# Fourteen small DMAs ahead of the direct copies of a sliding-window kernel

## The chip, the cores and the metric

The kernel runs on one core of one Trainium2 chip. The time is the device time of one execution in microseconds (us); a profiled execution also has a span, from its first to its last instruction. The core has 16 DMA engines. Two queues feed them here, one that SyncE (SP) issues to and one that ScalarE (ACT) issues to, and the profile lists them as q1 (SP) and q10 (ACT). No compute engine does any work on the data.

## The reference

The input is `x` of 32 batches, 4096 rows and 256 columns in float32. The result holds, for each batch, 127 windows of 64 rows that start every 32 rows:

```python
n_windows = (length - window_size) // stride + 1        # 127
for i in range(n_windows):
    start = i * stride
    result[:, i] = x[:, start:start + window_size].copy()
```

It is a pure copy. One block is 32 rows of 256 numbers, 32 KB, and it lies in one piece in memory. A window is two neighbouring blocks, 64 KB, also in one piece in `x` and in `out`. Neighbouring windows overlap by one block, so the result is twice as large as the input: 266.3 MB are written.

## The kernel before, in words

The 32 batches are divided between two paths, each with a queue of its own; the two share nothing but the 16 DMA engines and the memory.

**Direct** (class `Direct`, lines 36 to 57, on SP's queue) does the first 21 batches from memory to memory. `windows` (line 42) issues one DMA for `n` windows. Its outer dimension is the window, its inner one the 64 KB of a window, and `max_dma_last_dim` cuts the inner one into pieces: 16 KB where `size` is `DIRECT`, 32 KB where it is `2 * DIRECT`. `run` (line 52) does, for each batch, seven DMAs of 16 windows (112 windows, four pieces of 16 KB each) and then a remainder of 15 windows in two pieces of 32 KB each (line 57). That makes 147 DMAs of 16 windows and 21 remainders. No wait stands between them: SP issues as fast as its queue takes them.

**Staged** (class `Staged`, lines 60 to 107, on ACT's queue) does the last 11 batches over on-chip memory. A load (line 79) brings 16 blocks of 32 KB into one of 24 slots, one block in each of 16 partitions. A store (line 91) writes each slot twice, once as the first half of 16 windows and once as the second half of the windows before them. At the ends of a batch one of the two has only 15 blocks, which is 22 of the 176 stores. `run` (line 101) issues ten loads ahead (`LEAD`), then in turn one load and the two stores of an earlier slot. A load of a slot that is used again waits for both stores of it, and a store waits for its load.

Every DMA that nothing else waits for adds 16 to the semaphore `done` (`count`, line 31), and SP waits for the sum of these at the end (line 131).

The order of the work is the order of the program text on each queue; nothing plans it. Direct's first DMA is the one of windows 0 to 15 of batch 0, and batch 0's remainder is its eighth.

Of the kernel before, what the change touches and what calls it, by code (L numbers as in the profile page):

```python
# [1 line left out]

# [4 lines left out]


DIRECT, STAGE = 16384, 16384
N_STAGED = 11  # L10
N_TILES = 6
LEAD = 10


class Geometry:


    def __init__(self, tc, x, out, B, L, D, W, S, n_win):
        assert W == 2 * S and L % S == 0 and n_win == L // S - 1
        self.x, self.out = x, out  # L20
        self.blk, self.nb, self.nw = S * D, L // S, n_win
        self.done, self.total = tc.alloc_semaphore("done"), 0

    def xap(self, b, block, dims):
        return bass.AP(self.x.tensor, self.x.offset + (b * self.nb + block) * self.blk, dims)

    def oap(self, b, w, half, dims):
        at = ((b * self.nw + w) * 2 + half) * self.blk
        return bass.AP(self.out.tensor, self.out.offset + at, dims)

    def count(self, dma):
        dma.then_inc(self.done, 16)
        self.total += 16


class Direct:


    def __init__(self, g, batches):
        self.g, self.batches = g, batches  # L40

    def windows(self, q, b, w0, n, size):
        g = self.g
        g.count(
            q.dma_start(
                out=g.oap(b, w0, 0, [[2 * g.blk, n], [1, 2 * g.blk]]),
                in_=g.xap(b, w0, [[g.blk, n], [1, 2 * g.blk]]),
                max_dma_last_dim=size,
            )
        )  # L50

    def run(self, q):
        full = self.g.nw // 16 * 16
        for b in self.batches:
            for w0 in range(0, full, 16):
                self.windows(q, b, w0, 16, DIRECT)
            self.windows(q, b, full, self.g.nw - full, 2 * DIRECT)


class Staged:  # L60

    def __init__(self, g, tc, pool, dtype, batches, n_tiles):
        self.g = g
        tiles = [pool.tile([128, g.blk], dtype, name=f"xb{i}") for i in range(n_tiles)]
        self.slots = [t[32 + c : 96 : 4, :] for t in tiles for c in range(4)]
        self.loaded = [tc.alloc_semaphore(f"loaded{i}") for i in range(len(self.slots))]  # L70
        self.stored = [tc.alloc_semaphore(f"stored{i}") for i in range(len(self.slots))]
        self.groups = [(b, j) for b in batches for j in range(0, g.nb, 16)]

    def load(self, q, r):
        g, (b, j) = self.g, self.groups[r]
        n, i = divmod(r, len(self.slots))
        if n:
            q.wait_ge(self.stored[i], 32 * n)
        q.dma_start(
            out=self.slots[i], in_=g.xap(b, j, [[g.blk, 16], [1, g.blk]]),  # L80
            max_dma_last_dim=STAGE,
        ).then_inc(self.loaded[i], 16)

    def store(self, q, r):
        g, (b, j) = self.g, self.groups[r]
        n, i = divmod(r, len(self.slots))
        q.wait_ge(self.loaded[i], 16 * (n + 1))
        for half in (0, 1):
            lo = 1 if half and j == 0 else 0
            hi = 15 if not half and j + 16 == g.nb else 16  # L90
            dma = q.dma_start(
                out=g.oap(b, j + lo - half, half, [[2 * g.blk, hi - lo], [1, g.blk]]),
                in_=self.slots[i][lo:hi, :],
                max_dma_last_dim=STAGE,
            )
            if r + len(self.slots) < len(self.groups):
                dma.then_inc(self.stored[i], 16)
            else:
                g.count(dma)

    def run(self, q, lead):
        for r in range(lead):
            self.load(q, r)
        for r in range(len(self.groups)):
            if r + lead < len(self.groups):
                self.load(q, r + lead)
            self.store(q, r)


@with_exitstack  # L110
def kernel(
    ctx: ExitStack,
    tc: tile.TileContext,
    x: bass.AP,
    window_size: bass.AP,
    stride: bass.AP,
    out: bass.AP,
):
    nc = tc.nc
    W, S = int(window_size), int(stride)  # L120
    B, L, D = x.shape
    n_win = (L - W) // S + 1
    assert out.shape == (B, n_win, W, D)
    g = Geometry(tc, x, out, B, L, D, W, S, n_win)
    pool = ctx.enter_context(tc.tile_pool(name="xb", bufs=1))
    staged = Staged(g, tc, pool, x.dtype, range(B - N_STAGED, B), N_TILES)
    direct = Direct(g, range(B - N_STAGED))
    with tc.tile_critical():
        staged.run(nc.scalar, LEAD)
        direct.run(nc.sync)  # L130
        nc.sync.wait_ge(g.done, g.total)


# [1 line left out]
_INS = ['x', 'window_size', 'stride']  # L135
_OUTS = [((32, 127, 64, 256), 'float32')]

_NUMBERS = {'window_size': 64, 'stride': 32}


# [26 lines left out]
```

## Time and profile before

| What | Value |
|---|---|
| Time, median of 4 runs | 763.61 us (763.14 to 764.68) |
| The profiled execution's own time | 764.08 us |
| Its span | 762.3 us |
| Bytes moved by the DMA engines | 312.53 MB, mean 410 GB/s |
| Read from and written to the chip's memory | 220.92 MB and 266.34 MB, 639 GB/s over the span |
| Direct, SP's queue (q1) | 12705 packets, 174.80 MB |
| Staged, ACT's queue (q10) | 12606 packets, 137.71 MB |
| DMAs issued: direct of 16 windows, direct remainders | 147, 21 |
| DMAs issued: loads, stores of 16 blocks, stores of 15 blocks | 88, 154, 22 |
| Busy compute engines | POOL 0.2 us, four constants at the start |

A packet is one contiguous piece that one DMA engine moves, or the four bytes with which an engine adds to a semaphore after its part of a DMA. The DMA line of the profile cuts the span into 40 slices and gives the mean busy share of the 16 engines, in tenths. In a table of stretches of time the share is given in hundredths: 0.94 is what 15 busy engines of 16 make, 0.06 is one of 16. A share slightly over 1 is possible because the records of one packet and the next on an engine overlap by a few ns.

### The profile page before, as it was taken

Reading aid. Unit: us, or ns where it says so; the run is one execution under the profiler, and the core shown is the slowest. Engines: PE = TensorE matmul, PEld = TensorE weight load, DVE = VectorE, ACT = ScalarE, POOL = GpSimd, SP = SyncE. Lnnn points to the kernel's source line nnn. Section 1 sums busy time; section 2 is a strip of 40 time slices with the busy share of each in tenths; the row PEclk is TensorE's granted clock in tenths of the full one; section 3 lists DMA queues with packets and bytes.
Section 4 is the critical chain, followed back from the end, with each engine's and each line's share of the span. In section 5 each row is a group of like instructions: output and inputs, shape, how many; then the busy total and the mean of one; then the engine's idle time right before and its main releaser. Section 6 shows DMA issues by size and latency. Waiting matters only on the chain. (4 is left out here: it accounts for less than half of the span.)

```text
span 762.3 us, 482 instructions
## 1 busy us (share of the span) xinstructions
POOL 0.2 (0%) x4
## 2 busy tenths in 40 slices
POOL 0000000000000000000000000000000000000000
DMA  8999999999999999999999999999999999999993
GB/s 355 425 397 414 420 423 419 414 426 422 421 417 429 412 426 414 419 416 427 421 417 421 416 420 416 422 418 419 417 425 416 419 417 415 418 417 411 403 407 166
DMA packets 25314, 312.53 MB, mean 410 GB/s; under 512 B 6869, under 2 KB 6869, under 8 KB 6869
## 3 DMA queue, kind: packets, MB, share of 16 engines
q1 hardware_dynamic: 12705, 174.80, 55.0%
q10 hardware_dynamic: 12606, 137.71, 43.5%
q14 instruction: 3, 0.02, 0.0%
HBM read 220.92 MB, written 266.34 MB: 639 GB/s over the span
## 5 line engine op out<-in xcount | busy, mean ns | idle before, releaser
L148 POOL MEMSET const-uint8-127<- 128x1 uint8 x1 | 0.1, 102 | 0.0
L148 POOL MEMSET const-bfloat16-1.0<- 128x1 bf16 x1 | 0.1, 101 | 0.0
L148 POOL MEMSET const-float32-0.0<- 128x1 f32 x1 | 0.1, 98 | 0.2 <-issue 0.2
L148 POOL MEMSET const-float32-1.0<- 128x1 f32 x1 | 0.1, 98 | 0.0
## 6 DMA issues: line engine op xcount, KB each, us to landing
out_dram<-in_x_dram SPq DMA_DIRECT2D x147, 1024.0 KB, 70.4
out_dram<-xb ACTq DMA_DIRECT2D x154, 512.0 KB, 69.5
xb<-in_x_dram ACTq DMA_DIRECT2D x88, 512.0 KB, 72.7
out_dram<-in_x_dram SPq DMA_DIRECT2D x21, 960.0 KB, 68.9
out_dram<-xb ACTq DMA_DIRECT2D x22, 480.0 KB, 69.9
```

Source lines behind the costliest of these rows:

```text
L148: nc = _bacc.Bacc("TRN2", target_bir_lowering=False, num_devices=1)
```

## The change

Batch 0's remainder of 15 windows, one DMA before, is taken out of its place and put ahead of everything else on SP's queue, cut into 15 DMAs. A window `w0 + i` (i from 0 to 13) is cut into seven pieces of 512 numbers (2 KB) and a rest of 12800 numbers (50 KB). Seven DMAs copy piece c (c from 0 to 6) of the first 14 - 2c windows. Six more copy piece c (c from 1 to 6) of the last 2c of the 14 windows, which the first seven had left. The next one copies the rest of the 14 windows. A last one copies window 14, whole, with pieces of up to 32 KB. The bytes copied are the same as before, each once. Staged is untouched.

```diff
+STEP = 512
...
+    def rows(self, q, b, w0, n, r0, size):
+
+        g = self.g
+        g.count(
+            q.dma_start(
+                out=g.oap(b, w0, 0, [[2 * g.blk, n], [1, size]], r0),
+                in_=g.xap(b, w0, [[g.blk, n], [1, size]], r0),
+            )
+        )
+
+    def stagger(self, q, b, w0):
+
+
+        for c in range(7):
+            self.rows(q, b, w0, 14 - 2 * c, c * STEP, STEP)
+        for c in range(1, 7):
+            self.rows(q, b, w0 + 14 - 2 * c, 2 * c, c * STEP, STEP)
+        self.rows(q, b, w0, 14, 7 * STEP, 2 * self.g.blk - 7 * STEP)
+        self.windows(q, b, w0 + 14, 1, 2 * DIRECT)
+
     def run(self, q):
         full = self.g.nw // 16 * 16
+        self.stagger(q, self.batches[0], full)
         for b in self.batches:
             for w0 in range(0, full, 16):
                 self.windows(q, b, w0, 16, DIRECT)
-            self.windows(q, b, full, self.g.nw - full, 2 * DIRECT)
+            if b != self.batches[0]:
+                self.windows(q, b, full, self.g.nw - full, 2 * DIRECT)
```

`xap` and `oap` (lines 24 and 27) get a last argument `skip`, an offset in numbers that is added to the address; it is 0 where it isn't given.

More of the change, by code (lines that the diff above doesn't have):

```diff
@@ L22, in __init__, with xap, oap @@
         self.done, self.total = tc.alloc_semaphore("done"), 0
-    def xap(self, b, block, dims):
-        return bass.AP(self.x.tensor, self.x.offset + (b * self.nb + block) * self.blk, dims)
-    def oap(self, b, w, half, dims):
+    def xap(self, b, block, dims, skip=0):
+        return bass.AP(self.x.tensor, self.x.offset + (b * self.nb + block) * self.blk + skip, dims)
+    def oap(self, b, w, half, dims, skip=0):
         at = ((b * self.nw + w) * 2 + half) * self.blk
-        return bass.AP(self.out.tensor, self.out.offset + at, dims)
+        return bass.AP(self.out.tensor, self.out.offset + at + skip, dims)
     def count(self, dma):
```

## The prediction

> **What bounds the kernel now.** I read the DMA lines of the page first, since no engine computes.
>
> ```profile
> DMA  8999999999999999999999999999999999999993
> GB/s 355 425 397 414 420 423 419 414 426 422 421 417 429 412 426 414 419 416 427 421 417 421 416 420 416 422 418 419 417 425 416 419 417 415 418 417 411 403 407 166
> ...
> q1 hardware_dynamic: 12705, 174.80, 55.0%
> q10 hardware_dynamic: 12606, 137.71, 43.5%
> ```
>
> The engines are busy from start to end, so only their work, its division and its slowness count. The packet counts say who has which work. A DMA of 16 windows puts 4 pieces and a semaphore packet on each of 16 engines; if a remainder of 15 windows puts 2 pieces and a semaphore packet on each of 15, the sum is 147 x 16 x 5 + 21 x 15 x 3 = 12705, the very count of q1. One engine has no remainder, and by the same count none of the 22 stores of 15 blocks.
>
> Then the ends of the queues: the waits of SP, the direct issues, and the start of the timeline.
>
> ```profile
> SPq L128 <- DMA out_dram<-xb: 65.3, 1, 65.3
> ```
> ```profile
> L45 SPq DMA_DIRECT2D out_dram<-in_x_dram x168: 595/4299/8874, 0.9 to 688.7; - x168
> ```
> ```profile
> 0.90 7.51 ACTq L79 DMA_DIRECT2D xb<-in_x_dram  x11
> 0.94 62.30 SPq L45 DMA_DIRECT2D out_dram<-in_x_dram  x28
> ```
>
> SP's last issue starts at 688.7 and then SP waits 65.3 us: issuing is far ahead of the engines. An issue takes 595 ns at least and 4299 at the median, where it waits for room in the queue. Last, stretches of time (length, POOL, clock, DMA share, GB/s):
>
> ```profile
> core 0: us, POOL busy (x), PEclk, DMA share, GB/s
> 5.00:60.00 55.00, 0.00 (x0) 1.00 1.01 410
> 60.00:200.00 140.00, 0.00 (x0) 1.00 1.01 420
> 200.00:680.00 480.00, 0.00 (x0) 1.00 1.01 419
> 700.00:740.00 40.00, 0.00 (x0) 1.00 0.94 403
> 740.00:745.00 5.00, 0.00 (x0) 1.00 0.97 413
> 745.00:750.00 5.00, 0.00 (x0) 1.00 0.77 331
> 750.00:755.00 5.00, 0.00 (x0) 1.00 0.31 134
> 755.00:760.00 5.00, 0.00 (x0) 1.00 0.06 26
> ```
>
> From 700 on the share is 15 of 16: the engine with less work is done. The other 15 stop one after another from 745 on, and in the last 5 us one engine alone works. **That one engine sets the end.** In the packet records its last packet ends at 760.4; the one before it stops at 755.6.
>
> The same records give the packet times. Most pieces of 16 KB take 611 ns and most of 32 KB 1213, so 16 KB cost 602 and a piece 9 more; a semaphore packet takes 9. Each of the 15 engines has 147 x (4 x 611 + 9) + 21 x (2 x 1213 + 9) + 264 x (2 x 611 + 9) = 736.7 us, less 4 ns of overlap for each of 1590 packets, 730.3. Over these times the slower packets add 303.3 us on 16 engines, 19.0 each. With 2.4 us to the first packet the mean end is 751.7; the last engine is 8.7 later. From the ends of the remainders, this lag grows through the whole run: first to last 3.4 us in the first remainder, 11.7 in the eleventh, 16.2 in the last (a piece's own 1.2 included).
>
> The slow packets are denser early: 410 GB/s between 5 and 60 us against 420 later, (1 - 410/420) x 55 = 1.3 us of each engine. That is where the engines are nearly in step.
>
> **What the Trainium skill says.** (1) "DMA: Bandwidth & Descriptors", "Why a DMA increments its semaphore by 16 and not by 1": a DMA uses the largest k up to 16 that divides its slowest dimension that isn't 1, on the lowest-numbered k engines. The count above agrees on k = 15; which engines they are no view shows. (2) The same page, "Queues, rings and completion order": each engine goes round between the queues it has work for, and each queue is consumed in order on each engine. The steady shares 55.0 and 43.5% fit. (3) The same page, "Latency and other measured facts": copies with large power-of-two row pitches slow down, which it puts, as an inference, to aliasing of streams in lock-step. Here neighbouring engines are 32 KB apart in reading and 64 KB in writing, smaller than its cases; the 1.3 us may be a trace of it. (4) The same section: engines 7 and 15 are usually slower, with a cause that it doubts. Engine 15 has less work here; a slow engine 7 would fit the one straggler.
>
> **The change part by part.** *Removed*: batch 0's remainder, 2 x 1213 + 9 = 2435 ns on engines 0 to 14. *Added*: by (1), thirteen 2 KB DMAs give engines 0 and 1 13 pieces each, 2 and 3 11, then 9, 7, 5, 3 and, for 12 and 13, 1; engines 14 and 15 get none. The trace has no 2 KB piece: 602/8 + 9 = 84 ns by the sizes it has, 93 with its semaphore packet. Below that nothing is left to gain; above, the page's round trip of 800 ns if pieces did not overlap. I take 93, as four-byte packets pass in 9. The 50 KB piece: 602 x 50/16 + 9 = 1890, and 9. The single window has no outer dimension, so its two 32 KB pieces make k = 2: 2 x 1213 / 2 + 9 = 1222 on engines 0 and 1 (if it were cut sixteen ways, 1.1 less there). Sums, less 2435:
>
> - engines 0, 1: 13 x 93 + 1899 + 1222 = 4330, **+1.90 us**
> - 2, 3: 1023 + 1899, +0.49; 4, 5: +0.30; 6, 7: +0.12
> - 8, 9: -0.07; 10, 11: -0.26; 12, 13: -0.44; 14: -2.44
>
> It matters only for the straggler: the 14 others have 4.8 us of room. Over 15 engines the mean is +0.1; for engine 7 it is +0.12.
>
> *Issue*: 15 DMAs x 0.6 us put SP's first large DMA from 0.94 to about 10 us. Nothing waits for it on SP. The cover is ACT: 11 loads in 7.5 us, each 2 x 611 ns of every engine, 13.4 us of work from 2.4 us on, and stores from 8.45 on. Without that cover the engines would stand for most of 9 us. ACT's path gets ahead meanwhile: direct moved 2.75 MB in the first 15 us; now it moves the remainder's 0.98 MB and, from 11 us on at its old pace, some 0.9. About 0.9 MB of direct more are left at the end, 2 us at 410 GB/s that run without staged packets beside them. In the tail before, direct already ran last (q10 ended at 756.1), with nearly no slow packets: nothing charged.
>
> *Moved in time*: steps of 2 x 93 = 0.19 us between pairs, 1.1 over all, before the first large DMA. It spreads engines that lay within about 0.5 us of each other. At most the early excess, 1.3 us, goes; later the engines are microseconds apart anyway. I take two thirds, -0.9, and +0.1 for the bytes.
>
> **Sum.** 762.3 - 0.9 + 0.1 = 761.5 of span, with the 1.8 outside it 763.3, that is 0.8 below the profiled 764.08; 763.61 - 0.8 = **762.8 us**. 0.2% (1.5 us) is about what can be told from no change, so this is "no change" by a little.
>
> **Rivals.** *The spread lasts* (chance 0.26). If the order in which engines reach the memory decides the slow packets all through, a fifth of the 19.0 us goes: 3.8, 759.8. For: the lag of the last engine grows steadily. Against: the spread of 3 to 16 us that arises by itself has not lowered the later excess further.
>
> *Engines 0 or 1 become last* (0.14), the slower side. Place: the opening on those two. Price: +1.9 us if the straggler is one of them, two in fifteen, 765.5. If it is another, they must lose more than their room: at least 4.8 us, which needs 2 KB pieces of (4.8 - 1.9)/13 = 0.22 us above my 93 ns; unpipelined at 0.8 they would cost 9 us more. Against: 9 ns packets.
>
> *Collisions fall otherwise* (0.12): the straggler's slow packets are rearranged by new phases and it loses 2 to 3 us more: 766.2. The four runs agree within 1.5 us, so chance from run to run is small, but it is a fixed pattern that the change redraws.
>
> *No separation* (0.06): the loads that fill the engines level it out, or k is otherwise; 763.6.
>
> **Chances and range.** The likeliest case has 0.42, its own range 761.6 to 764.4; of it 0.09 passes the 0.2% below. Faster 0.26 + 0.09 = 0.35; same 0.33 + 0.06 = 0.39; slower 0.14 + 0.12 = 0.26. The range leaves out a third of the lasting spread and, above, the costly 2 KB pieces and the worst rearranging: 758.8 to 766.4.
>
> **What would show it.** Packets of q1: 12705 - 45 + 2 x 98 + 28 + 4 = 12888; 2 KB packets near 84 ns; q1's first large packet near 11 us with the engines full; more than 410 GB/s between 5 and 60 us, the same 420 later; one engine alone at the end, a little earlier. I am wrong if GB/s after 60 us differs by more than 2, if 2 KB packets take over 0.3 us, or if two engines end together last.

## The result, and the profile after

The changed kernel is slower by 0.4%: 764.96 us median over 44 runs against 762.18 over 63 runs of the kernel before, a ratio of 1.004 with a 95% interval of 1.0029 to 1.005. The prediction had 762.8, and called it "no change" by a little. Single executions of either kernel scatter with a standard deviation of 1.8 to 1.9 us, so that the 763.61 of four runs that the prediction started from lay 1.4 us above the median of many. In what follows, times are compared by ratios. Each run has one profile, so a small difference between two profiles counts only where several runs show it.

The DMA lines and the queues of the changed kernel, on its page:

```profile
DMA  9999999999999999999999999999999999999994
GB/s 350 408 425 424 418 425 419 421 422 418 417 417 417 420 423 419 423 414 425 417 418 418 424 416 421 417 419 414 426 413 419 413 422 404 416 422 412 405 370 168
...
q1 hardware_dynamic: 12916, 174.80, 55.1%
q10 hardware_dynamic: 12606, 137.71, 43.5%
```

The engines are as busy as before, the bytes are the same, and of the late slices only the last full one stands out: 370 GB/s where it was 407. SP's queue has 28 packets more than the 12888 that I had worked out: the single window went out as 16 pieces of 4 KB on 16 engines, not as two of 32 KB on two (the packet records hold 16 packets of 4096 bytes).

The stretches of time (length, POOL, clock, DMA share, GB/s):

```profile
5.00:60.00 55.00, 0.00 (x0) 1.00 1.01 414
60.00:200.00 140.00, 0.00 (x0) 1.00 1.01 420
200.00:680.00 480.00, 0.00 (x0) 1.00 1.01 418
700.00:740.00 40.00, 0.00 (x0) 1.00 0.95 397
740.00:745.00 5.00, 0.00 (x0) 1.00 0.96 347
745.00:750.00 5.00, 0.00 (x0) 1.00 0.88 308
750.00:755.00 5.00, 0.00 (x0) 1.00 0.60 246
755.00:760.00 5.00, 0.00 (x0) 1.00 0.18 75
```

Up to 680 us the table is that of the kernel before, even a little better between 5 and 60. Then it parts. Between 740 and 745 the share is 0.96, as good as before's 0.97, yet the engines move 347 GB/s where they moved 413. Busy engines that move less have slow packets. By the packet records, the time above the usual 611 and 1213 ns is 21.72 us per engine against 18.96. Of the 2.76 us more, 2.57 lie after 700 us: 2.59 per engine in place of 0.02. The rest is small and of both signs: +0.29 before 15 us, -0.75 between 15 and 60, +0.67 from 60 to 700. The last of these says nothing: over the profiles of both paths together, the last experiment's apart, this stretch had from 13.8 to 17.3. From here on, "slow packets" means this time above the usual, per engine.

What runs there? The queues of the kernel before, from 720 us to its end (packets, MB, share of 16 engines):

```profile
DMA packets 1012, 12.55 MB, mean 292 GB/s; under 512 B 281, under 2 KB 281, under 8 KB 281
q1 hardware_dynamic: 553, 7.62, 41.4%
q10 hardware_dynamic: 459, 4.93, 27.0%
```

The same of the changed kernel:

```profile
DMA packets 957, 12.68 MB, mean 282 GB/s; under 512 B 243, under 2 KB 243, under 8 KB 243
q1 hardware_dynamic: 738, 10.36, 58.9%
q10 hardware_dynamic: 219, 2.33, 12.5%
```

At 720 us nearly as much is left as before (12.68 MB, 12.55), but of another kind: 2.7 MB more of direct and 2.6 MB less of staged. Staged's last packet ends at 743.1 us instead of 756.1; after it direct runs alone. The surplus is as old as the run. The queues of the kernel before from 2 to 15 us:

```profile
q1 hardware_dynamic: 200, 2.75, 51.4%
q10 hardware_dynamic: 206, 2.33, 47.4%
```

And of the changed kernel:

```profile
q10 hardware_dynamic: 418, 4.72, 93.6%
q1 hardware_dynamic: 169, 0.18, 5.1%
```

Direct moved 0.18 MB instead of 2.75: the lag of 2.6 MB is complete by 15 us and is still there at 720. The issues of the opening's line in the changed kernel (shortest, median and longest in ns, first and last start):

```profile
L57 SPq DMA_DIRECT2D out_dram<-in_x_dram x14: 566/716/1025, 1.0 to 10.7; - x14
```

And the timeline of its start (start, length, queue):

```profile
0.91 7.79 ACTq L102 DMA_DIRECT2D xb<-in_x_dram  x11
0.95 10.56 SPq L57 DMA_DIRECT2D out_dram<-in_x_dram  x14
...
11.56 52.51 SPq L46 DMA_DIRECT2D out_dram<-in_x_dram  x26
```

The second group of SP begins with the single window, so its first large DMA was issued near 12 us; the first 16 KB packet started at 16.8 us. Nothing repairs such a lag afterwards, and one line shows why. The queues of the kernel before between 60 and 680 us:

```profile
q1 hardware_dynamic: 10530, 144.89, 56.0%
q10 hardware_dynamic: 10528, 115.03, 44.6%
```

The packet counts are equal to 2 in 10,000, whatever the packets' sizes and semaphore packets included. Equal counts alone would also fit turns of several packets. The packet records decide: where just one packet starts within 6 ns before or 2 ns after the end of another, the two can be taken as neighbours on one engine. Of 12,716 such pairs between 60 and 680 us, 12,631 change the queue. So while both queues have work, an engine takes one packet from each in turn. The shares are set by that, and a queue that is behind stays behind.

### The profile page after: what moved, and what is told of

It reads as the page before. It is cut to its first block, busy times and chain, and to the rows that moved or that the text cites. A ratio compares the mean times of both kernels' runs of the same rounds, so it can differ in the third digit from the quotient of the medians.

```text
span 764.1 us, 496 instructions
## 1 busy us (share of the span) xinstructions
POOL 0.2 (0%) x4
```

## The experiments

**Theory Q** stood at the start: the opening puts direct behind, staged ends early, and the end, direct alone, is slow. Its **rivals** say that the opening itself costs, by its pieces or its uneven bytes on engines 0 and 1 (rival P) or by the collisions that it redraws (theory O). Rival I grants the lag, and puts it down to the late issue of SP's large DMAs instead of the turns. The texts set off below are what was expected before each run.

### The remainder moved to the front, whole

```diff
-        self.stagger(q, self.batches[0], full)
+        self.windows(q, self.batches[0], full, self.g.nw - full, 2 * DIRECT)
```

> The changed kernel with batch 0's remainder still first on SP's queue, but whole, as one DMA of 15 windows: the move alone, no small pieces. Theory Q (the queue): the small pieces take turns from SP's queue, so direct falls some 2.6 MB behind staged, staged ends some 13 us early and direct finishes alone, slowly. Without small pieces there is no lag: the time of the kernel before (ratio 0.998 to 1.002), q10's last packet near 756 us, mean slow-packet time after 700 us near 0 per engine. Theory O (the order): taking the remainder out of its place redraws which packets collide; then this costs the same 0.3 to 0.5% as the change.

Measured: 761.36 us, ratio 0.9986 (0.9971 to 1.000). Staged's last packet ends at 752.0, 4 us before the expected 756, and 0.03 us of slow packets per engine follow 700 us. The move alone costs nothing, so theory O has no support here.

### A lag without any pieces

The kernel before, and one line:

```diff
+        nc.sync.wait_ge(staged.loaded[6], 16)
         direct.run(nc.sync)
```

> The kernel before, but SP waits for the seventh staged load before its first DMA, so direct begins near 13 us; no small piece, no moved remainder. Theory Q: a lag of about 2.4 MB whatever its cause costs the same: ratio 1.002 to 1.005, q10 ends near 744 us, 2 to 3 us of slow packets per engine after 700 us. Rival P (pieces): what costs is the pieces themselves or the uneven bytes on engines 0 and 1; then the ratio is 0.998 to 1.002.

Measured: 767.11 us, ratio 1.0058 (1.0035 to 1.0081). Direct had moved nothing by 15 us and was 3.1 MB behind at 60; staged ended at 743.4; 2.95 us of slow packets per engine follow 700 us. Its stretches:

```profile
700.00:720.00 20.00, 0.00 (x0) 1.00 0.95 401
720.00:740.00 20.00, 0.00 (x0) 1.00 0.95 381
740.00:750.00 10.00, 0.00 (x0) 1.00 0.92 326
```

The last of these stretches in the changed kernel, and in the kernel before:

```profile
740.00:750.00 10.00, 0.00 (x0) 1.00 0.92 328
740.00:750.00 10.00, 0.00 (x0) 1.00 0.87 372
```

This is the changed kernel's tail without a single small piece. A lag of direct is enough for the whole loss; pieces aren't needed.

### The opening in the remainder's own place

```diff
-        self.stagger(q, self.batches[0], full)
...
             if b != self.batches[0]:
                 self.windows(q, b, full, self.g.nw - full, 2 * DIRECT)
+            else:
+                self.stagger(q, b, full)
```

> The 15 DMAs of the opening stand where the remainder stood, behind batch 0's seven large DMAs, so SP's first large DMA is issued at 1 us again. Theory Q says that an engine takes one packet from each queue in turn, a semaphore packet too, so that 228 packets instead of 45 still cost direct 183 turns of 12.8 KB, 2.3 MB: ratio 1.002 to 1.005, q10 ends near 745. Rival I (issue): it is the ten us in which SP issues small DMAs that put direct behind; then the lag is gone here, ratio 0.998 to 1.002, q10 ends near 756.

Measured: 0.9978 (0.9966 to 0.9991), outside the ranges of both. Staged's end was at 748.6 and the slow packets after 700 us 0.88 per engine, between the two expectations: at 60 us direct was 1.1 MB behind and staged 1.4 MB ahead, not 2.3. I had worked out the turns badly. With the single window as 16 packets the opening has 256 packets in place of 45, not 228, so 211 turns are given away, not 183. In these staged moves 211 x 10.9 KB (115.03 MB by 10528 packets), 2.3 MB, but in the same time it would have moved 44% of that anyway, so it gains 56%, 1.3 MB. With that the size fits, though it was worked out after the result. By subtraction, the other half of the changed kernel's 2.6 MB comes from the first twelve us, in which SP had issued nothing large.

The ratio below 1 was tried again, on another chip, together with a variant that splits the pieces between the queues (below).

> The kernel with all small pieces in the remainder's own place once more, beside the one with the pieces on both queues. The first time it had 0.9978 although staged ended early and 0.9 us of slow packets followed after 700 us, which Theory M counts as a loss. If 0.9978 was real, 0.996 to 0.999 again, and below its neighbour; if it was chance, 0.999 to 1.002.

Measured: 1.001 (0.9993 to 1.0026), with 1.05 us of slow packets after 700. So 0.9978 did not repeat: about the time of the kernel before, in agreement with a lag of about half. The two intervals of this one kernel don't overlap. A single ratio can thus be off by some 0.2 or 0.3% beyond what its interval says, and a loss of that size, as in the next two experiments, is read from the packets rather than from the time.

### Giving the lag back

ACT takes over batch 0's first three large DMAs, right after its ten loads:

```diff
+MOVED = 3
...
+        self.moved = [(batches[0], 16 * i) for i in range(MOVED)]
+
+    def extra(self, q):
+        for b, w0 in self.moved:
+            self.windows(q, b, w0, 16, DIRECT)
...
             for w0 in range(0, full, 16):
-                self.windows(q, b, w0, 16, DIRECT)
+                if (b, w0) not in self.moved:
+                    self.windows(q, b, w0, 16, DIRECT)
...
         for r in range(lead):
             self.load(q, r)
+        extra(q)
```

> The changed kernel with its whole opening, but ACT issues batch 0's first three DMAs of 16 windows (3.1 MB) right after its ten loads, instead of SP. That gives the 2.6 MB back to direct and holds staged up as much. Theory Q: the time of the kernel before or a little less (ratio 0.996 to 1.001), q10 ends at 755 us or later, hardly any slow packets after 700. Rivals P and O (pieces, uneven bytes, redrawn collisions): still 1.003 to 1.005.

Measured: 1.0023 (1.0011 to 1.0036); staged's queue ended at 757.6. The stretches:

```profile
15.00:60.00 45.00, 0.00 (x0) 1.00 1.01 382
60.00:680.00 620.00, 0.00 (x0) 1.00 1.01 419
...
740.00:750.00 10.00, 0.00 (x0) 1.00 0.93 397
```

The tail is mended (397 GB/s at 0.93, 0.03 us of slow packets after 700), as theory Q said, but the time isn't. The loss has moved: 382 GB/s between 15 and 60 us where the changed kernel has 420. That is where direct DMAs are now on both queues, with little of staged between them; slow packets there are 5.03 us per engine instead of 1.19. (With ACT's 3.1 MB, 12.2 of the stretch's 17.2 MB are direct.) Theory Q as I had put it, that the leftover queue is the trouble, was too narrow. I split it in two. **Theory M**: the memory can't serve direct alone at full speed, wherever and on whichever queue it runs. **Theory U**: it is one queue left over that is slow.

### The last direct DMAs on ACT's queue

With the same `extra` and the same exception in `run`:

```diff
+        self.moved = [(batches[-1], w0) for w0 in (64, 80, 96)]
...
         staged.run(nc.scalar, LEAD)
+        direct.extra(nc.scalar)
```

> The changed kernel, but the last three direct DMAs of 16 windows of the last batch are issued by ACT, behind its last stores: both queues then end together, yet the traffic of the last 20 us is still direct alone. Theory M (the memory): packets are slow while direct runs without staged beside it, on whichever queue; ratio 1.002 to 1.006, 2 us or more of slow packets per engine after 700 us. Theory U (uneven queues): the loss comes from one queue being left over; then the ratio is 0.998 to 1.001 and the slow packets after 700 are gone.

Measured: 1.0024 (1.0011 to 1.0038). Both queues ended within 0.2 us of each other (757.6 and 757.8 in the profiled execution), and still:

```profile
720.00:740.00 20.00, 0.00 (x0) 1.00 0.95 382
740.00:750.00 10.00, 0.00 (x0) 1.00 0.87 315
```

2.54 us of slow packets per engine after 700, as in the changed kernel. Two even queues don't help when both carry direct, so theory U falls. It falls by these packets: the loss in time is perhaps smaller than the change's, though the intervals overlap, and the profiled execution was the fastest of the 22 (761.47 us), as it had fewer slow packets between 60 and 700 us, 13.8 us against 16.0 before.

### Each path by itself

One profile each, of the kernel before without the call of the other path. The first leaves the staged batches unwritten (first line below), the second the direct ones (second line).

```diff
-        staged.run(nc.scalar, LEAD)
...
-        direct.run(nc.sync)
```

> The kernel before with the staged path left out, so the last 11 batches are not written: what direct costs by itself. By packets of 611 and 1213 ns an engine has 411.7 us, less 3.2 of overlap; with the start and the end 415 us. Theory M: the packets are slow as in the last stretch of the changed kernel, where 0.92 of the engines moved 328 GB/s against 0.87 and 372 before, 17% less for a busy engine: 470 to 500 us. Theory U: 413 to 425 us.

> The kernel before with the direct path left out, so the first 21 batches are not written. An engine has 264 x 1231 ns = 325 us, less 3.2; with the start and the end 328 us. Theory M: few slow packets, 327 to 335 us, so that a stretch of staged alone earns nothing back. If staged alone is slow too, 340 us or more, then a lead of either path costs and Theory M is only half of it.

Direct alone took 540.33 us, staged alone 349.56. The page of direct alone:

```profile
q1 hardware_dynamic: 12705, 174.80, 98.1%
...
HBM read 174.78 MB, written 174.78 MB: 649 GB/s over the span
```

And two of its stretches:

```profile
60.00:200.00 140.00, 0.00 (x0) 1.00 1.00 329
200.00:300.00 100.00, 0.00 (x0) 1.00 1.00 328
```

All 16 engines are busy and move 328 GB/s, 656 GB/s of reads and writes together. This is the rate of the tails between 740 and 750 us: 328 in the changed kernel, 326 with SP's wait, 315 in the last experiment, though fewer engines were busy there. The end of direct alone, where its engines stop one after another, shows the same:

```profile
505.00:519.00 14.00, 0.00 (x0) 1.00 0.94 325
527.00:533.00 6.00, 0.00 (x0) 1.00 0.75 309
```

Fifteen busy engines move what sixteen do, and twelve nearly as much. So it is not a rate per engine, as the expectation had taken it, but a ceiling for all of them together, and the loss is larger than expected (540 us, not 470 to 500). Now the mixture between 60 and 680 us can be read anew: direct counts twice in memory traffic, (2 x 144.89 + 115.03) MB / 620 us = 653 GB/s. **The mixture stands at about the same 650 GB/s of memory traffic, and at full engines besides.** In act_first3, the run with direct on both queues early, the slow stretch from 15 to 60 us comes to (17.2 + 12.2) MB / 45 us = 653 GB/s as well. So direct has too much memory traffic per byte to run alone at the mixture's rate, and staged dilutes it. That the ceiling is one of reads plus writes is inferred from this agreement; no run changed the traffic per byte in another way.

Staged alone needed 349.56 us where the packets' usual times make 328, beyond the 340 that I had set as the mark. Its page:

```profile
q10 hardware_dynamic: 12606, 137.71, 97.7%
...
HBM read 46.14 MB, written 91.55 MB: 396 GB/s over the span
```

And its stretch between start and end:

```profile
60.00:330.00 270.00, 0.00 (x0) 1.00 0.99 401
```

So staged alone is slower than the mixture too, by a little; why, at 401 GB/s of traffic, no run here tells. A lead of either path costs, though not alike. As an estimate, a megabyte costs 1/328 - 1/419 = 0.66 us when it is direct that runs alone, and 1/401 - 1/419 = 0.11 us when it is staged. For 2.6 MB of each that is 2.0 us of the 2.8 us that the medians differ by.

### The mirror image

ACT issues the opening, and SP starts with its large DMAs at once:

```diff
+        direct.stagger(nc.scalar, direct.batches[0], n_win // 16 * 16)
         staged.run(nc.scalar, LEAD)
...
-        self.stagger(q, self.batches[0], full)
```

> The changed kernel, but ACT issues the 15 DMAs of the opening ahead of its loads, and SP starts with its large DMAs at once: the mirror image, with staged behind and direct ahead. Theory M (direct alone is held by the memory to the 325 to 329 GB/s that direct_alone showed): direct runs alone in the first ten us, at about 330 GB/s, and staged ends last with hardly a slow packet after 700 us; the loss is paid at the front: ratio 1.001 to 1.005. Rival L (only the lag of direct hurts, since the end is where it shows): with direct ahead the ratio is 0.995 to 1.000.

Measured: 1.0041 (1.0025 to 1.0056). The stretches:

```profile
5.00:15.00 10.00, 0.00 (x0) 1.00 0.97 325
15.00:60.00 45.00, 0.00 (x0) 1.00 1.01 397
...
740.00:750.00 10.00, 0.00 (x0) 1.00 0.95 405
```

The first two of these in the kernel before:

```profile
5.00:15.00 10.00, 0.00 (x0) 1.00 1.00 403
15.00:60.00 45.00, 0.00 (x0) 1.00 1.01 412
```

Direct is ahead here, SP's queue ends at 750.7 and ACT's at 761.1, and 0.03 us of slow packets follow 700 us. The loss is as large as the change's and stands at the front: 325 GB/s and 397, and before 60 us 6.1 us of slow packets per engine against 2.9. Rival L falls: it isn't the end that is slow, it is direct without staged.

### Pieces on both queues

In the remainder's place, with the six DMAs of the second group issued by ACT behind its first stores:

```diff
+    def second(self, q):
+        b, w0 = self.batches[0], self.g.nw // 16 * 16
+        for c in range(1, 7):
+            self.rows(q, b, w0 + 14 - 2 * c, 2 * c, c * STEP, STEP)
...
             self.store(q, r)
+            if r == 0:
+                extra(q)
```

> The small pieces in the remainder's own place, with the six DMAs of the second group on ACT behind its first stores and the rest on SP, so that both queues give up turns and neither gets ahead. Theory M: the 0.9 us of slow packets after 700 us that the kernel with all pieces in place on SP had go, ratio 0.995 to 0.998 if the separation of the engines is worth the 0.7 us that the profiles show between 15 and 60 us; 0.998 to 1.000 if that was chance. Above 1.001 Theory M is missing something.

> The kernel with the pieces in place on both queues, on the same chip as its neighbour: by Theory M at or below it, 0.997 to 1.001, with less than 0.1 us of slow packets after 700 us against some 0.9.

Measured: 1.0011 (0.9998 to 1.0024), and on another chip 1.0001 (0.9985 to 1.0017), with 0.02 and 0.03 us of slow packets after 700 us. Neither queue gets ahead, and the time is that of the kernel before. The first ratio lies just above the 1.001 that I had set as the mark, with an interval that holds 1. The separation of the engines, which is all that is left of the change here, has no gain that can be measured. The slow packets between 15 and 60 us were 2.55 and 2.30 us per engine, not below the 1.94 of before; with all pieces on SP in place they were 1.29 and 1.30. What lowered them there and in the changed kernel is open: separation, or less direct traffic in that stretch.

### An attempt on the idle engine

The kernel before, with 16 batches' remainders cut across the batches, so that they use 16 engines:

```diff
+    def across(self, q, b, w):
+        g, size = self.g, 2 * self.g.blk
+        g.count(
+            q.dma_start(
+                out=g.oap(b, w, 0, [[2 * g.nw * g.blk, 16], [1, size]]),
+                in_=g.xap(b, w, [[g.nb * g.blk, 16], [1, size]]),
...
-            self.windows(q, b, full, self.g.nw - full, 2 * DIRECT)
+            if b < 15:
+                self.across(q, 0, full + b)
+            elif b > 15:
+                self.windows(q, b, full, self.g.nw - full, 2 * DIRECT)
```

> The kernel before, with the remainders of the first 16 batches cut the other way: after each of batches 0 to 14 one DMA of the same window of 16 batches, which uses 16 engines, where 15 windows of one batch used 15. Engines 0 to 14 have one remainder less, 2.4 us; engine 15, which stood idle from 680 on, has 15 more. If the straggler's load is what sets the end: ratio 0.996 to 0.998. If the 4 MB between neighbouring engines' reads makes them collide, 1.000 to 1.01.

Measured: 1.0142 (1.0121 to 1.0164), 34.3 us of slow packets per engine against 19.0, and 386 GB/s between 5 and 60 us. The better division is more than lost. A memory that is simply full doesn't explain it: between 20 and 40 us the engines were as busy as before, yet the memory had 546 GB/s of reads and writes (3.93 MB of direct, counted twice, and 3.06 of staged in 20 us) where the kernel before had 649. Something slows these packets below the ceiling. That reads 4 MB apart collide is a guess that fits; no run varied the distance.

No version beat the kernel before in a way that repeated.

## Why the prediction was wrong

**What bounds the kernel.** Half right. The work per engine, the early end of the engine with less work and the one straggler were read correctly. What I missed is a second bound of nearly the same height. Both numbers were at hand: the page's 639 GB/s of reads and writes, and 410 GB/s of packets. Direct alone at 419 GB/s would need 838 GB/s. The Trainium skill's "HBM Reference", "Specifications (TRN2)", gives 716 GB/s for the memory of a core pair. Half of that, 358 GB/s, is an estimate from the page of the most that direct could move by itself, and it alone would have put a price on direct running last. direct_alone's measured 649 GB/s of reads and writes is 91% of the page's figure.

**The step that failed** is the one called *Issue*. It said that some 0.9 MB of direct would be left at the end, and: "In the tail before, direct already ran last (q10 ended at 756.1), with nearly no slow packets: nothing charged." Both halves were wrong. The lag was 2.6 MB. Direct's first 16 KB packet came at 16.8 us, not near 11, and of the opening's own 0.98 MB, which the sum took as moved by 15 us, only the small pieces were: direct had moved 0.18 MB in all, since each small packet used up a turn of its queue and the 50 KB packets began at 15.4 us. The price wasn't nothing: 2.59 us of slow packets per engine after 700 us. The tail before was no evidence for a price of zero, because after 756 us one engine was left (a share of 0.06), which doesn't fill the memory; at 740 us the two queues still ran side by side.

**The cover** held as such: ACT's loads kept the engines full in the opening (a share of 0.98 between 5 and 15 us). I asked only whether they stood still, not what the cover used up. It used up 2.6 MB of staged's work, which was needed later to dilute direct.

**Turns.** The prediction took from the Trainium skill ("DMA: Bandwidth & Descriptors", "Queues, rings and completion order") that engines go round between the queues, and compared it with shares of time. The page has an engine drain about 9 to 17 descriptors before it switches; in this trace it switched after every packet record (12,631 of 12,716 pairs). With that unit, 256 packets in place of 45 are 211 turns given away.

**Pieces.** Right: 91 of the 98 small packets took 82 to 84 ns, as priced; seven took 185 to 576. Uneven bytes: the single window went to 16 engines, so engines 0 and 1 had 13 x 93 + 1899 + 168 - 2435 = +0.84 us, not +1.90. The prediction had named this other case.

**Moved in time.** The sum had the pieces spread the engines by 1.1 us. By the packet records the 98 small packets start from 3.8 to 17.1 us, each waiting for its turn. The gain of 0.9 us came out at about half: 0.75 less of slow packets between 15 and 60 us, 0.29 more before. Its cause isn't shown, and split between the queues the pieces brought none. No run ties the early excess to lock-step.

**Rivals.** None of them had the mechanism. The two slower cases, engines 0 or 1 becoming last and collisions that fall otherwise, were given for other reasons. That 764.96 lies within the range is luck: the range was wide, and it reached up for these reasons.

## What to carry to other kernels

Where two paths share the DMA engines, add up what each asks of the memory per byte moved. A path that is slower alone than in the mixture, as direct was here (328 GB/s against 419), should have the other beside it from its first byte to its last. Both paths should then start and end together, whichever queue they are on: a head start of staged was paid for at the end, one of direct at once. Where engines alternate between queues by packets, as here, count the packets: small pieces take turns, not only bytes. And work that "hides" a delay is work spent: ask what it will be missing from. All this was worth 0.4% here.

## What was unexpected of the hardware

- Copies from memory to memory on 16 busy engines moved 328 GB/s, 656 GB/s of reads and writes; mixed with copies over on-chip memory the engines moved 419 GB/s at 653 GB/s of reads and writes. With 15 engines copies from memory to memory moved 325 GB/s, with 12 still 309.
- Between 60 and 680 us the two queues had 10530 and 10528 packets, and 12,631 of 12,716 neighbouring packets that can be told change the queue: an engine's turn was one packet, of 16 KB or of 4 bytes.
- One window of 64 KB with a cap of 32 KB, one row, went out as 16 packets of 4 KB, 159 ns each.
- The first 16 KB packet of SP's queue started about 5 us after its DMA could be issued, where the kernel before had 3.1 us (0.94 to 4.04); no run looked into that.
